# Two queue steps a job in the first output pair, later turns, and a last residual by ScalarE and an accumulating transfer

## The chip, the cores and the metric

The kernel runs on one core of a Trainium2 chip. The metric is the device time of one launch in microseconds. A few terms: TensorE (PE in the profile) multiplies matrices, VectorE (DVE) and ScalarE (ACT) work on elements, GpSimd (POOL) does some small arithmetic and issues DMAs, and SyncE (SP) issues the other DMAs. Each engine works through its own queue of instructions in order. An instruction waits for what it needs, and everything queued behind it on that engine waits too.

## The reference

Two layers, batch 1, 512 tokens (S), 2048 features (D), all in float32:

```python
def hybrid_layer(x, w_in, w_out, g_pre, g_post, ...):
    h = rmsnorm(x, g_pre)
    z = h @ w_in                            # 2048 x 7184
    gq, gk, gv, gg, ga, aq, ak, av, ag = split_columns(z)
    ...
    o_gla = gla_chunk_causal(...)           # 4 heads, gated linear attention
    o_gla = rmsnorm(o_gla, g_gla) * silu(gg)
    o_att = chunk_band_attention(...)       # 8 heads, band of 9 chunks of 64
    o_att = rmsnorm(o_att, g_att) * silu(ag)
    y = concatenate([o_gla, o_att]) @ w_out # 2048 x 2048
    return x + rmsnorm(y, g_post)           # the residual of this case
```

The two large projections, `w_in` and `w_out`, are most of the work.

## The kernel before

**Jobs.** All weights pass through one stream of jobs. A job is one piece of a weight block: 256 input rows by 512 columns, kept as a 128x1024 tile. For each job SyncE loads the piece (512 KB) into `raw` or `H`; where a sum or difference of two pieces is wanted, VectorE forms it (`H` at L185, `raw` at L187); ScalarE makes a rounded high part `wh` (L191); VectorE makes the rest, `wl` (L199). TensorE then multiplies high by high, high by low and low by high: 12 matmuls of 128x512 a job (L381). There are three `wl` tiles and four of each of the other kinds. `ahead` prepares loads, high parts and low parts for the next few jobs after each job's matmuls.

**Pairs.** `fast_gemm` multiplies a pair of weight blocks in seven products of four jobs each instead of eight (P1, P5, P6, P3, P7, P2, P4 in the order of the input pairs; the output pairs have their own order), in the manner of Winograd's form of Strassen's method. It works on sums of the operands (tiles `sa`, loaded from DRAM) as well as on the operands themselves (`a` or `g`). When a product is complete, `finished` calls the pair's consumer once per half of columns and pair of token tiles. The consumer gets a sum, formed by VectorE at L338 from TensorE's accumulator and a kept copy `ev` (L333).

**Side work.** What isn't a job stands in two lists: `tasks`, generators that do one step at a time, and `delayed`, entries with a counter of steps. `pump(n)` advances both by n steps. A `Pace` object calls it after every job with a given rate, so rate 1 is one step a job and rate 3 three. `until` and `drain` pump out of turn.

**The gate pair and the first output pair.** The last pair of input blocks (`PAIRS[5]`) gives the GLA gate. `gg_consume` applies SiLU on ScalarE, multiplies the normalised head outputs on VectorE (L1249; tiles `bias` and `sg`), and puts one `turn_gla` per head and half in `delayed`. A turn transposes the head's output on TensorE (L1164), and splits it into high and low parts on ScalarE and VectorE (L105, L106). The turned parts are operands of the output projection; the task `output_sums` forms their sums and stores them to DRAM. The pair W01 (columns 0 to 1023 of `w_out`) follows in both layers, at rate 1, with consumer `out_consume(0)`. In layer 0 the pair W23 then goes through `std_gemm`, in layer 1 (the last) through `fast_gemm` at rate 3, with `lag=3`.

**Residual.** `project` squares and sums the projected row on ScalarE (L1280) and multiplies it by the gain on VectorE (L1281). When all 2048 columns of a token tile t (128 tokens) are there, `finish_token` reduces the sums on VectorE (L1294), takes them to the power -1/2 on GpSimd (`rsqrt`, L421), and forms x + r*y on VectorE in one step a half (L1306), in place over the loaded residual. It then stores the row (L1308). In the last layer, tokens 0 and 1 are finished by the task `finish(0, ...)` while the last product still runs, and 2 and 3 behind it; token 3 goes in four parts of 512 columns, the fourth by ScalarE and GpSimd. `load_tokens` loads the residual from `x_mid`, a DRAM buffer, with GpSimd's queue (L456), after W01: 1024 columns a tile for tokens 0 to 2, and 512 for token 3 (tiles `bias` and `sg`).

**What sets the order.** The program is written without fixed instruction orders: a scheduler that plans by estimated durations sets each engine's queue order within the data dependences and the reuse of tiles.

Of the kernel before, what the change touches and what calls it, by code (L numbers as in the profile page):

```python
# [11 lines left out]
ALU = mybir.AluOpType  # L12
# [3 lines left out]
P = 128  # L16
# [4 lines left out]
NT = S // P  # L21
# [12 lines left out]
def hybrid_trunk(  # L34
# [653 lines left out]
    def layer(l):  # L688
# [471 lines left out]
        def turn_gla(h, p):  # L1160
            ps = aux()
            for f in range(2):
                for tt in range(2):
                    nc.tensor.transpose(  # L1164
                        ps[:, f * 256 + tt * P : f * 256 + (tt + 1) * P],
                        normed[h, p][:, tt, f * P : (f + 1) * P], ident,
                    )
# [72 lines left out]
        def gg_consume(j, h, t, src, comb):  # L1240
            if t == 0:
                until(lambda: len(gla_done) == 4 and (j or {(1, 2), (1, 3)} <= set(og)))
                for i in range(2):
                    out_parts(2 * j + i)
            sg = t2()
            nc.scalar.activation(sg, settled(src, comb), AF.Silu)
            for i in range(2):
                dst = normed[2 * j + i, h][:, t, :]
                nc.vector.tensor_tensor(out=dst, in0=dst, in1=sg[:, i * 256 : (i + 1) * 256], op=ALU.mult)  # L1249
                if t:  # L1250
                    delayed.append([(8 + 3 * i if j else 6 + i if h == 0 else 3 + i), lambda hd=2 * j + i: turn_gla(hd, h)])

        tasks.append(output_sums())
        fast_gemm(l, PAIRS[5], gg_consume, rate=3, after=fetch_operands)
# [30 lines left out]
        def out_evac(n):  # L1285
# [3 lines left out]
                project(o, n, ps, gp)  # L1289
            return f  # L1290

        def finish_token(t, xs):
            s1, r = sm(1), sm(1)
            nc.vector.tensor_reduce(out=s1, in_=ssy[t], axis=mybir.AxisListType.X, op=ALU.add)  # L1294
            rsqrt(r, s1)
            yield
            end = last and t == NT - 1
            step = 512 if end else xs[0].shape[-1]
            for i in range(D // step):
                h, o = i * step // 1024, i * step % 1024  # L1300
                xt, yt = piece(xs, i * step, step), ys[t, h][:, o : o + step]
                if end and i == 3:
                    nc.scalar.activation(yt, yt, AF.Copy, scale=r)
                    nc.gpsimd.tensor_tensor(out=xt, in0=yt, in1=xt, op=ALU.add)
                else:
                    nc.vector.scalar_tensor_tensor(out=xt, in0=yt, scalar=r, in1=xt, op0=ALU.mult, op1=ALU.add)  # L1306
                q = (nc.sync, nc.scalar)[i % 2] if last and t > 1 else nc.gpsimd
                q.dma_start((out if last else x_mid)[t * P : (t + 1) * P, i * step : (i + 1) * step], xt)  # L1308
                yield

        def finish(pair, xs):
            for j in range(2):
                yield from finish_token(2 * pair + j, xs[j])
# [8 lines left out]
        def out_consume(n):  # L1322
            if n:
                gains[:] = [load_gain(n + j, t2()) for j in range(2)]

            def f(j, h, t, src, comb):
# [11 lines left out]
        fast_gemm(l, W01, out_consume(0), rate=1, after=lambda k, c: used.add((k, c)), end=True, ops=O)  # L1338
# [72 lines left out]
```

## Time and profile before

| | |
|---|---|
| median of 3 runs | 1658.23 us (1656.5 to 1661.95) |
| profiled execution | 1657.88 us, span of the trace 1656.1 us |
| mean granted TensorE clock | 0.994 |
| DMA over the span | 256 GB/s, read 371.32 MB, written 53.23 MB |

A row of a timeline has start and duration in us, engine, source line, operation, tiles (out<-in) and sizes, the number of instructions, and in brackets the idle time before them with the tile or transfer that ended it. A row of waits has the waiting instruction, what it waited for, the sum in us, the count and the longest. A row of windows gives a stretch (from:to), its length, and each engine's busy time with its number of instructions, then the granted clock of TensorE, the busy share of the 16 DMA engines and GB/s. Times in brackets of a timeline row are idle time of that engine and not necessarily lost time of the kernel. Issue instructions of DMAs are listed but not counted as busy.

### The profile page before, as it was taken

Reading aid. Unit: us, or ns where it says so; the run is one execution under the profiler, and the core shown is the slowest. Engines: PE = TensorE matmul, PEld = TensorE weight load, DVE = VectorE, ACT = ScalarE, POOL = GpSimd, SP = SyncE. Lnnn points to the kernel's source line nnn. Section 1 sums busy time; section 2 is a strip of 40 time slices with the busy share of each in tenths; the row PEclk is TensorE's granted clock in tenths of the full one; section 3 lists DMA queues with packets and bytes.
Section 4 is the critical chain, followed back from the end, with each engine's and each line's share of the span. In section 5 each row is a group of like instructions: output and inputs, shape, how many; then the busy total and the mean of one; then the engine's idle time right before and its main releaser. Section 6 shows DMA issues by size and latency. Waiting matters only on the chain.

```text
span 1656.1 us, 24554 instructions
## 1 busy us (share of the span) xinstructions
PE 1623.9 (98%) x8986; PEld 1386.1 (84%) x8986; DVE 1260.1 (76%) x1639; ACT 905.3 (55%) x1494; POOL 131.7 (8%) x200
## 2 busy tenths in 40 slices
PE   9999999999999999999999999999999999998996
PEld 7888999998887777788888889999988877776785
DVE  5977677687688769986785676787766878788778
ACT  7554445566554546555773444465665545565442
POOL 0110000000100110001022000000100000012002
PEclk9999999999999999999999999999999999999998
DMA  8898685885859677386689496858768586876975
GB/s 343 272 349 305 220 302 184 295 286 177 302 186 345 214 253 259 104 309 226 219 310 399 141 330 205 299 174 295 243 206 281 201 317 212 288 252 209 350 230 202
DMA packets 130616, 426.17 MB, mean 257 GB/s; under 512 B 14068, under 2 KB 26740, under 8 KB 130496
## 3 DMA queue, kind: packets, MB, share of 16 engines
q1 hardware_dynamic: 113184, 363.99, 63.5%
q0 software_dynamic: 16736, 59.53, 9.7%
q8 instruction: 71, 1.16, 0.3%
q10 hardware_dynamic: 576, 1.08, 0.2%
q14 instruction: 49, 0.40, 0.1%
HBM read 371.32 MB, written 53.23 MB: 256 GB/s over the span
## 4 chain that ended last, share of the span: by engine, by line
PE 88%; DVE 5%; DMA 3%; issue 2%; ACT 0%; POOL 0%; DVEq 0%; ACTq 0%; POOLq 0%
PE mm L381 42%; PE mm L371 18%; PE mm L302 16%; DMA raw<-in_w_dram 3%; PE ax L891 2%; DVE wl L199 2%; PE ax L381 1%; PE ax L1072 1%; PE ax L874 1%; PE ax L711 1%; PE ax L1044 1%; DVE H L185 1%; PE ax L855 1%; PE ax L854 1%; PE ax L853 1%
## 5 line engine op out<-in xcount | busy, mean ns | idle before, releaser
L381 PE MATMUL mm<-wh,sa 128*128 128x512 f32 x1472 | 479.5, 396 | 4.0 <-ACT wh L191 4.0
L191 ACT CAST wh<-raw 128x1024 fp32r<-128x1024 f32 (+1 forms) x253 | 265.0, 1052 | 245.5 <-PE mm L381 63.1
L199 DVE TENSOR_TENSOR wl<-raw,wh 128x1024 fp32r<-128x1024 f32 (+1 forms) x253 | 306.6, 1215 | 97.5 <-PE mm L381 40.8
L191 ACT CAST wh<-H 128x1024 fp32r<-128x1024 f32 x240 | 251.6, 1051 | 235.3 <-PE mm L381 94.7
L199 DVE TENSOR_TENSOR wl<-H,wh 128x1024 fp32r<-128x1024 f32 x240 | 292.3, 1220 | 95.7 <-PE mm L381 30.0
L381 PEld LDWEIGHTS mm<-wh,sa 128*128 128x128 f32 x1472 | 277.1, 189 | 72.5 <-issue 8.3
L381 PE MATMUL mm<-wl,sa 128*128 128x512 f32 x736 | 290.1, 394 | 5.6 <-DVE wl L199 5.5
L371 PE MATMUL mm<-sa,wh 128*128 128x256 f32 x1280 | 236.8, 285 | 0.5 <-DMA sa<-S 0.5
L381 PE MATMUL mm<-wh,a 128*128 128x512 f32 x608 | 201.3, 396 | 0.0
L371 PEld LDWEIGHTS mm<-sa,wh 128*128 128x128 f32 x1280 | 199.6, 191 | 0.7 <-ACT wh L191 0.6
L371 PE MATMUL mm<-sa,wl 128*128 128x256 f32 x640 | 181.4, 283 | 0.5 <-DVE wl L199 0.5
L381 PEld LDWEIGHTS mm<-wl,sa 128*128 128x128 f32 x736 | 139.1, 189 | 35.5 <-DVE wl L199 8.5
L185 DVE TENSOR_TENSOR H<-H,raw 128x1024 f32<-128x1024 f32 x132 | 160.1, 1217 | 8.5 <-DMA raw<-in_w_dram 7.4
L381 PEld LDWEIGHTS mm<-wh,a 128*128 128x128 f32 x608 | 113.8, 189 | 23.5
L381 PE MATMUL mm<-wl,a 128*128 128x512 f32 x304 | 120.4, 396 | 3.9 <-DVE wl L199 3.9
L187 DVE TENSOR_TENSOR raw<-H,raw 128x1024 f32<-128x1024 f32 x60 | 73.4, 1224 | 65.7 <-DMA raw<-in_w_dram 65.6
L371 PEld LDWEIGHTS mm<-sa,wl 128*128 128x128 f32 x640 | 122.5, 191 | 1.0 <-DVE wl L199 0.7
L421 POOL TENSOR_TENSOR sm<-sm,mhalf 128x2 f32<-128x2 f32 (+2 forms) x42 | 52.7, 1255 | 793.8 <-DVE sm L901 452.8
L371 PE MATMUL mm<-a,wh 128*128 128x256 f32 x512 | 95.2, 285 | 0.0
L381 PE MATMUL mm<-wh,g 128*128 128x512 f32 x288 | 92.2, 395 | 0.0
L302 PE MATMUL mm<-wh,a 128*128 128x512 f32 x288 | 91.7, 390 | 0.0
L333 ACT COPY ev<-mm 128x512 f32<-128x512 f32 x96 | 55.7, 583 | 50.7 <-PE mm L381 33.9
(236 smaller groups left out, 2435.0 us busy)
## 6 DMA issues: line engine op xcount, KB each, us to landing
raw<-in_w_dram SPq DMA_DIRECT2D x323, 512.0 KB, 4.8
sa<-S SPq DMA_DIRECT2D x184, 512.0 KB, 4.3
H<-in_w_dram SPq DMA_DIRECT2D x60, 512.0 KB, 4.7
sa<-A SPq DMA_DIRECT2D x48, 512.0 KB, 6.0
S<-g POOLq DMA_DIRECT2D x32, 512.0 KB, 9.3
sa<-oS SPq DMA_DIRECT2D x16, 512.0 KB, 5.2
oa<-g POOLq DMA_DIRECT2D x12, 512.0 KB, 6.3
bias<-in_rel_dram SPq DMA_DIRECT2D x16, 256.0 KB, 3.2
```

Of the source, the lines that this page charges most:

```text
L185: nc.vector.tensor_tensor(out=h, in0=h, in1=r, op=ALU.add)
L187: nc.vector.tensor_tensor(out=r, in0=h, in1=r, op=ALU.subtract)
L191: last_cast[0] = nc.scalar.copy(self.wh[:, z, :], src[:, z, :]).ins
L199: nc.vector.tensor_tensor(out=self.wl[:, z, :], in0=self.src[:, z, :], in1=self.wh[:, z, :].bitcast(F32), op=ALU.subtract)
L302: nc.tensor.matmul(pss[o], a(part, kk, o) if callable(a) else a[:, part, t], rhs[:, kk, :], start=(i == 0 and kk == 0 and m == 0), stop=(i ...
L333: nc.scalar.copy(e, src[t])
L371: nc.tensor.matmul(dst, lhs[:, kk, f], a[:, part, tok], start=(fresh and kk == 0 and m == 0 and ft % 2 == 0), stop=(c == 3 and kk == 1 and ...
L381: nc.tensor.matmul(out_ps[t], a[:, part, tok], rhs[:, kk, :], start=(fresh and kk == 0 and m == 0), stop=(c == 3 and kk == 1 and m == 2), ...
L421: nc.gpsimd.tensor_tensor(out=out_r, in0=v, in1=mhalf[:, : v.shape[-1]], op=ALU.pow)
L711: nc.tensor.matmul(ps[0:96, half * 256 : (half + 1) * 256], wga[kt // 10][:, kt % 10, :], op[:, i, (kt % 2) * 256 : (kt % 2 + 1) * 256], s ...
L853: nc.tensor.matmul(ps[:, :n], self.qh[:, t], self.kh[:, :n], start=True, stop=False)
L891: nc.tensor.matmul(o, self.pt[i][:, j * P : (j + 1) * P], av[hd // 4, j // 2][:, j % 2, (hd % 4) * P : (hd % 4 + 1) * P], start=(j == 0), ...
```

## The change

Three things change.

1. The turns of the gate pair: their step counts become 8 for the first head of a pair and 11 for the second, in every half; before these were 8 and 11 only for heads 2 and 3, and 6 and 7, or 3 and 4, for heads 0 and 1.
2. The pair W01 advances the side work by two steps a job instead of one, in both layers.
3. In the last layer, tokens 0 and 1 (both halves) and the first half of token 2 are scaled by r in place by ScalarE (L1305 of the changed kernel). A DMA from GpSimd's queue adds the row of `x_mid` to it (L1306), and SyncE stores it (L1307). The loads of x_mid of tokens 0 and 1, four of 512 KB, are dropped; those of tokens 2 and 3 stay. Both tokens 2 and 3 are reduced first (L1296). Then VectorE does the second half of token 2, held behind the reduction of token 3 by `issue_after`, and all four parts of token 3 (L1311).

```diff
-                    delayed.append([(8 + 3 * i if j else 6 + i if h == 0 else 3 + i), lambda hd=2 * j + i: turn_gla(hd, h)])
+                    delayed.append([8 + 3 * i, lambda hd=2 * j + i: turn_gla(hd, h)])
...
-            nc.vector.tensor_reduce(out=s1, in_=ssy[t], axis=mybir.AxisListType.X, op=ALU.add)
+            reduced[t] = nc.vector.tensor_reduce(out=s1, in_=ssy[t], axis=mybir.AxisListType.X, op=ALU.add).ins
             rsqrt(r, s1)
             yield
-            end = last and t == NT - 1
-            step = 512 if end else xs[0].shape[-1]
+            step = 512 if t == NT - 1 else 1024
             for i in range(D // step):
                 h, o = i * step // 1024, i * step % 1024
-                xt, yt = piece(xs, i * step, step), ys[t, h][:, o : o + step]
-                if end and i == 3:
+                yt = ys[t, h][:, o : o + step]
+                rows = slice(t * P, (t + 1) * P), slice(i * step, (i + 1) * step)
+                if last and (t < 2 or (t == 2 and i == 0)):
                     nc.scalar.activation(yt, yt, AF.Copy, scale=r)
-                    nc.gpsimd.tensor_tensor(out=xt, in0=yt, in1=xt, op=ALU.add)
+                    nc.gpsimd.dma_start(yt, x_mid[rows], accum_op=ALU.add)
+                    nc.sync.dma_start(out[rows], yt)
                 else:
-                    nc.vector.scalar_tensor_tensor(out=xt, in0=yt, scalar=r, in1=xt, op0=ALU.mult, op1=ALU.add)
-                q = (nc.sync, nc.scalar)[i % 2] if last and t > 1 else nc.gpsimd
-                q.dma_start((out if last else x_mid)[t * P : (t + 1) * P, i * step : (i + 1) * step], xt)
+                    xt = piece(xs, i * step, step)
+                    with tc.issue_after(reduced[3]) if last and t == 2 else nullcontext():
+                        nc.vector.scalar_tensor_tensor(out=xt, in0=yt, scalar=r, in1=xt, op0=ALU.mult, op1=ALU.add)
+                    q = (nc.sync, nc.scalar)[i % 2] if last else nc.gpsimd
+                    q.dma_start((out if last else x_mid)[rows], xt)
                 yield
...
                     if (j, h) == (0, 1):
-                        for _ in finish_token(o, xs[1][t]):
-                            pass
+                        ends.append(finish_token(o, xs[1][t]))
+                        next(ends[-1])
+                        if t:
+                            for end in ends:
+                                for _ in end:
+                                    pass
...
-        fast_gemm(l, W01, out_consume(0), rate=1, ...)
+        fast_gemm(l, W01, out_consume(0), rate=2, ...)
         drain()
-        xs.extend(load_tokens(half, x_src, nc.gpsimd) for half in range(2))
+        xs.extend(None if last and half == 0 else load_tokens(half, x_src, nc.gpsimd) for half in range(2))
```

The order of instructions moves in three places. The first is TensorE's queue in layer 0 at the end of the gate pair. Its last jobs write `mm_...`; jobs that write `ax_...` with operand `g_...` belong to W01; rows from `cst` are a turn's transposes. Before:

```order
L381 MATMUL mm_6653<-wh_6589,a_1119_5935 128x512
L381 MATMUL mm_6654<-wh_6589,a_1119_5935 128x512
L1164 MATMUL ax_6593<-cst,bias_6053 128x128
L1164 MATMUL ax_6629<-cst,sg_6227 128x128
L1164 MATMUL ax_6593<-cst,bias_6053 128x128 x3
L1164 MATMUL ax_6629<-cst,sg_6227 128x128 x3
L381 MATMUL mm_6653<-wl_6615,a_1119_5935 128x512
```

And now:

```order
L381 MATMUL mm_6629<-wh_6589,a_1119_5935 128x512
L381 MATMUL mm_6630<-wh_6589,a_1119_5935 128x512
L1164 MATMUL ax_6619<-cst,bias_6053 128x128
L1164 MATMUL ax_6651<-cst,sg_6227 128x128
L381 MATMUL ax_6661<-wh_6551,g_1221_6394 128x512
L381 MATMUL ax_6662<-wh_6551,g_1221_6394 128x512
L381 MATMUL ax_6661<-wl_6587,g_1221_6394 128x512
...
L381 MATMUL ax_6662<-wh_6607,g_1226_6423 128x512
L1164 MATMUL ax_6619<-cst,bias_6053 128x128 x3
L1164 MATMUL ax_6651<-cst,sg_6227 128x128 x3
L381 MATMUL mm_6629<-wl_6605,a_1119_5935 128x512
```

A whole job of W01 (12 matmuls with `wh_6551` and `wl_6587`) and the first two matmuls of its next job now stand between the first two transposes and the other six. The matmul with `wl_6605`, which was `wl_6615`, comes after them. Layer 1 has the same move at the same place.

The second is VectorE's queue in layer 1, at the end of the gate pair and the start of W01. L338 forms a sum out of an accumulator, L1281 is the gain, L106 is part of a turn or of `output_sums`. Before:

```order
L185 TENSOR_TENSOR H_14427<-H_14427,raw_14652 128x1024
L338 TENSOR_TENSOR t_2866_14743<-ax_14503,ev_14609 128x512
L1281 TENSOR_TENSOR a_2868_14747<-t_2866_14743,bias_14494 128x512
L338 TENSOR_TENSOR t_2870_14751<-ax_14504,ev_14611 128x512
L199 TENSOR_TENSOR wl_14695<-H_14427,wh_14674 128x1024
L106 TENSOR_TENSOR g_2856_14679<-g_2789_14363,g_2856_14679 128x512
L1281 TENSOR_TENSOR a_2872_14755<-t_2870_14751,bias_14494 128x512
L185 TENSOR_TENSOR H_14482<-H_14482,raw_14676 128x1024
L199 TENSOR_TENSOR wl_14719<-H_14482,wh_14698 128x1024
```

And now:

```order
L185 TENSOR_TENSOR H_14417<-H_14417,raw_14652 128x1024
L338 TENSOR_TENSOR t_2866_14743<-ax_14469,ev_14609 128x512
L185 TENSOR_TENSOR H_14457<-H_14457,raw_14676 128x1024
L1281 TENSOR_TENSOR a_2868_14747<-t_2866_14743,bias_14552 128x512
L338 TENSOR_TENSOR t_2870_14751<-ax_14470,ev_14611 128x512
L199 TENSOR_TENSOR wl_14695<-H_14417,wh_14674 128x1024
L106 TENSOR_TENSOR g_2856_14679<-g_2789_14363,g_2856_14679 128x512
L1281 TENSOR_TENSOR a_2872_14755<-t_2870_14751,bias_14552 128x512
L199 TENSOR_TENSOR wl_14719<-H_14457,wh_14698 128x1024
```

The sum that needs the load `raw_14676` stood behind `wl_14695` and both gains; it now stands ahead of them.

The third is ScalarE's queue in the last product of the last layer. `wh` rows are casts for the last four jobs, L1280 is the square of a projected row. Before:

```order
L1280 ACTIVATE t_3048_15569,ssy_14745<-t_3047_15567 128x512
L191 COPY wh_15600<-H_15013 128x1024
L1280 ACTIVATE t_3050_15574,ssy_14753<-t_3049_15572 128x512
L191 COPY wh_15627<-H_15069 128x1024
L191 COPY wh_15646<-H_15105 128x1024
L191 COPY wh_15665<-H_15181 128x1024
```

And now, with `sm_15570` and `sm_15599` the powers of tokens 0 and 1 from GpSimd:

```order
L191 COPY wh_15594<-H_15013 128x1024
L1280 ACTIVATE t_3046_15566,ssy_14753<-t_3045_15564 128x512
L1305 ACTIVATE a_2868_14747<-a_2868_14747,sm_15570 128x1024
L1305 ACTIVATE g_2991_15303<-g_2991_15303,sm_15570 128x1024
L191 COPY wh_15623<-H_15069 128x1024
L1305 ACTIVATE a_2872_14755<-a_2872_14755,sm_15599 128x1024
L1305 ACTIVATE g_2994_15309<-g_2994_15309,sm_15599 128x1024
L191 COPY wh_15642<-H_15105 128x1024
L191 COPY wh_15661<-H_15173 128x1024
```

Four scalings stand between the casts, two ahead of `wh_15623` and two ahead of `wh_15642`. On VectorE the four residual steps that stood between the last `wl` rows are gone. On GpSimd each power is now followed by its accumulating transfers; the one for token 2 comes after both last powers.

More of the change, by code (lines that the diff above doesn't have):

```diff
@@ L1290, in out_evac @@
             return f
+        reduced = {}
         def finish_token(t, xs):
             s1, r = sm(1), sm(1)
[L1294 removed]
+            reduced[t] = nc.vector.tensor_reduce(out=s1, in_=ssy[t], axis=mybir.AxisListType.X, op=ALU.add).ins
             rsqrt(r, s1)
             yield
[L1297 to L1298 removed]
+            step = 512 if t == NT - 1 else 1024
             for i in range(D // step):
                 h, o = i * step // 1024, i * step % 1024
[L1301 to L1302 removed]
+                yt = ys[t, h][:, o : o + step]
+                rows = slice(t * P, (t + 1) * P), slice(i * step, (i + 1) * step)
+                if last and (t < 2 or (t == 2 and i == 0)):
                     nc.scalar.activation(yt, yt, AF.Copy, scale=r)
[L1304 to L1308 removed]
+                    nc.gpsimd.dma_start(yt, x_mid[rows], accum_op=ALU.add)
+                    nc.sync.dma_start(out[rows], yt)
+                else:
+                    xt = piece(xs, i * step, step)
[3 more added lines that the diff above has]
+                    q.dma_start((out if last else x_mid)[rows], xt)
                 yield
@@ L1312, in finish @@
             for j in range(2):
-                yield from finish_token(2 * pair + j, xs[j])
+                yield from finish_token(2 * pair + j, xs and xs[j])
             if not last:
@@ L1324, in out_consume @@
                 gains[:] = [load_gain(n + j, t2()) for j in range(2)]
+            ends = []
             def f(j, h, t, src, comb):
@@ L1333, in f @@
                     if (j, h) == (0, 1):
-                        for _ in finish_token(o, xs[1][t]):
-                            pass
+                        ends.append(finish_token(o, xs[1][t]))
[4 more added lines that the diff above has]
+                                    pass
             return f
-        fast_gemm(l, W01, out_consume(0), rate=1, after=lambda k, c: used.add((k, c)), end=True, ops=O)
+        fast_gemm(l, W01, out_consume(0), rate=2, after=lambda k, c: used.add((k, c)), end=True, ops=O)
         drain()
-        xs.extend(load_tokens(half, x_src, nc.gpsimd) for half in range(2))
+        xs.extend(None if last and half == 0 else load_tokens(half, x_src, nc.gpsimd) for half in range(2))
         if last:
```

## The prediction

> **What bounds the kernel now.** The page comes first: busy time by engine, the kinds of instruction that feed TensorE, and then the list of what TensorE waits for.
>
> ```profile
> PE 1623.9 (98%) x8986; PEld 1386.1 (84%) x8986; DVE 1260.1 (76%) x1639; ACT 905.3 (55%) x1494; POOL 131.7 (8%) x200
> L191 ACT CAST wh<-raw 128x1024 fp32r<-128x1024 f32 (+1 forms) x253 | 265.0, 1052 | 245.5 <-PE mm L381 63.1
> L199 DVE TENSOR_TENSOR wl<-H,wh 128x1024 fp32r<-128x1024 f32 x240 | 292.3, 1220 | 95.7 <-PE mm L381 30.0
> PE mm L381 <- DVE wl L199: 13.3, 12, 2.1
> PE mm L381 <- ACT wh L191: 4.0, 3, 2.1
> ```
>
> TensorE is busy for 1623.9 of 1656.1 us. The change takes no matmul away, so it can only win in the 32 us in which TensorE stands still, or where it runs at half pace. Of these, 17.3 us are waits for the two halves of a weight block, and the last 12 lie behind the last matmul. So the question is which of those waits fall in the first output pair and in the tail. The timeline of TensorE from the last jobs of the gate pair to the middle of the first output pair shows them, layer 0 first, then layer 1:
>
> ```profile
> 647.38 0.39 PE L381 MATMUL mm<-wh,a 128*128 128x512 f32 x1
> ...
> 651.16 0.55 PE L1164 MATMUL ax<-cst,bias 128*128 128x128 f32 x3 [0.22 <-DVE bias L1249]
> 653.84 0.50 PE L381 MATMUL mm<-wl,a 128*128 128x512 f32 x1 [1.79 <-DVE wl L199]
> 687.09 0.50 PE L381 MATMUL mm<-wl,sa 128*128 128x512 f32 x1 [2.10 <-DVE wl L199]
> 691.72 0.74 PE L381 MATMUL mm<-wh,sa 128*128 128x512 f32 x2 [1.56 <-ACT wh L191]
> 700.22 0.39 PE L381 MATMUL mm<-wl,g 128*128 128x512 f32 x1
> 1473.54 0.50 PE L381 MATMUL mm<-wl,a 128*128 128x512 f32 x1 [1.79 <-DVE wl L199]
> 1508.44 0.50 PE L381 MATMUL mm<-wl,sa 128*128 128x512 f32 x1 [2.01 <-DVE wl L199]
> 1514.69 0.74 PE L381 MATMUL mm<-wh,sa 128*128 128x512 f32 x2 [2.11 <-ACT wh L191]
> 1515.95 0.80 PE L381 MATMUL mm<-wl,sa 128*128 128x512 f32 x1 [0.52 <-DVE wl L199]
> 1525.77 0.39 PE L381 MATMUL mm<-wl,g 128*128 128x512 f32 x1
> ```
>
> Both layers have the same three stalls: 1.79 us between the gate pair's last jobs, 2.0 to 2.1 us at the first wl of the third product, and 1.6 to 2.1 us at the wh after that. VectorE's own windows over these stretches, and what VectorE waits for in them, say how much could be had:
>
> ```profile
> 652.57:687.09 34.52, 32.02 (x43) 1.00 0.47 153
> 686.95:700.22 13.27, 11.41 (x13) 1.00 0.16 47
> 1472.29:1508.44 36.15, 32.19 (x43) 0.95 0.63 212
> 1508.44:1525.77 17.33, 11.72 (x13) 0.80 0.56 209
> DVE wl L199 <- ACT g L105: 1.6, 1, 1.6
> DVE H L185 <- DMA raw<-in_w_dram: 2.7, 1, 2.7
> ```
>
> The columns are length, VectorE's busy time and instructions, granted clock, share of DMA and GB/s. VectorE, not TensorE, is nearly full here: its idle time is 34.52 - 32.02 = 2.50 and 1.86 us in layer 0 (4.36 in all), and 3.96 and 5.61 us in layer 1 (9.57). No reordering gains more than that here while VectorE's work stays what it is.
>
> **Part 1: the first output pair at two steps a job, turns later.** Neither edit adds or drops an engine's work; they reorder. TensorE now runs a whole job of the output pair, 12 matmuls, before the six remaining transposes and the wl that it waited 1.79 us for. The cover costs nothing: its weight block is one that both kernels need.
>
> Layer 0. The early stall of 0.22 + 1.79 us is filled by that job. What decides after it is VectorE's queue up to the wl at 687.09. Of the 2.50 us of idle time there, 1.61 were a wait for ScalarE's copy of a turn (L105); the turns now come later, behind weight blocks that stand ready, so I let this go and keep the rest, a wait for a sum in TensorE. That is 1.6 us. Of the following 1.86 us, a wait for wh, I take a quarter, 0.4. Sum: **2.0 us** (ends 1.0, part of the first alone, and 4.4, all idle time).
>
> Layer 1. The first stretch is built alike: **2.0 us**. The second takes 1525.77 - 1508.44 = 17.33 us where layer 0's (687.09 to 700.22) takes 13.13 for the same jobs. The excess of 4.2 us has three sources in the rows: a DMA wait of 2.67 us on VectorE, wh late by 0.55 us more than in layer 0 (2.11 against 1.56) with 0.52 us of wl behind it, and a granted clock of 0.80. If the weight blocks run ahead, layer 0 shows what the stretch costs, so I take the **4.2 us**. It is the softest term (0 to 4.2): in the changed order the sum H that waited for that DMA stands ahead of another wl on VectorE, so that the same late load would now hold more.
>
> The dropped loads of x_mid belong here. Two of the six rows of such loads, their landing times, and the stretch they fall in:
>
> ```profile
> 1525.53 0.53 POOL L456 DMA_DIRECT2D g<-x_mid  x1
> 1527.51 0.53 POOL L456 DMA_DIRECT2D g<-x_mid  x1 [0.24 <-issue]
> g<-x_mid POOLq DMA_DIRECT2D x6, 512.0 KB, 9.4
> 1526.00:1563.00 37.00, 34.19 (x146) 26.52 (x144) 28.53 (x31) 17.07 (x26) 3.26 (x7) 1.00 0.99 375
> ```
>
> From 1526 to 1563 the DMA engines are full (0.99, 375 GB/s) and TensorE is idle for 37.00 - 34.19 = 2.8 us. Four loads of 512 KB go in all, two of them here: 1.05 MB at 375 GB/s is 2.8 us less to move. The weight loads share the path only in part and the stretch ends full anyway; I take **0.8** of the 2.8 us. Layer 1 in all: 2.0 + 4.2 + 0.8 = **7.0 us** (ends 2.0 and 9.6 + 2.8 = 12.4).
>
> **Part 2: the last layer's residual.** In the last jobs TensorE, VectorE and GpSimd look like this:
>
> ```profile
> 1631.09 0.50 PE L381 MATMUL mm<-wl,g 128*128 128x512 f32 x1 [2.11 <-DVE wl L199]
> 1635.53 0.40 PE L381 MATMUL mm<-wl,g 128*128 128x512 f32 x1
> 1638.62 0.50 PE L381 MATMUL mm<-wl,g 128*128 128x512 f32 x1 [0.17 <-DVE wl L199]
> 1643.52 0.39 PE L381 MATMUL mm<-wh,g 128*128 128x512 f32 x1
> 1627.36 1.28 DVE L1306 SCALAR_TENSOR_TENSOR g<-a,sm,g 128x1024 f32<-128x1024 f32 x1 [0.47 <-POOL sm L421]
> 1629.82 1.21 DVE L199 TENSOR_TENSOR wl<-H,wh 128x1024 fp32r<-128x1024 f32 x1
> 1624.17 3.15 POOL L421 TENSOR_TENSOR sm<-sm,mhalf 128x1 f32<-128x1 f32 x1 [55.62 <-DVE sm L1294]
> 1648.78 0.54 POOL L421 TENSOR_TENSOR sm<-sm,mhalf 128x1 f32<-128x1 f32 x1 [2.73 <-DVE sm L1294]
> ```
>
> VectorE stops 0.47 us for GpSimd's power, does two residual steps (2 x 1.28), and only then the wl that TensorE waits 2.11 us for. Four such steps leave VectorE before the last matmul, about 5 us. TensorE can win 2.11 + 0.17 us; and the 12 matmuls after the first stall take 1635.53 - 1631.09 = 4.44 us, where the 22 from 1638.62 to 1643.52 start 0.23 us apart, which makes 2.8 for 12: 1.6 us lost. Together 3.9. But ScalarE's scalings (its price by the nearest row, a cast of the same size, is 1.05 us) now stand in ScalarE's queue ahead of three wh casts, and wait for the power. VectorE no longer stops for that power: it took 3.15 us under back-to-back VectorE steps against 0.54 alone. I take half, **2.0 us** (ends -0.9 and 3.9).
>
> The Trainium skill, "SBUF — State Buffer", section Who interferes with whom, says that a VectorE instruction with two SBUF inputs contends with a GpSimd instruction that reads SBUF, and that the second fully blocks. By that rule the power waits for one VectorE step at most, 1.22 us, and with its own 0.54 would be there 1.4 us sooner than in 3.15: the sum below would be 1646.3. The 3.15 us are more than two such steps, so the measured wait is the longer one.
>
> Behind the last matmul. Before: from 1643.91 to the end at 1656.1, 12.2 us. After, the branch of token 2's first half is: sums and the power, about 2.1 us (1645.12 + 0.93 in the rows below), scaling 1.05, the accumulating transfer issued behind the last power, so about 3.9 us after the last matmul, its landing, then and the store from SyncE.
>
> ```profile
> 1645.12 0.93 POOL L421 TENSOR_TENSOR sm<-sm,mhalf 128x1 f32<-128x1 f32 x1 [6.85 <-DVE sm L1294]
> 1649.35 1.42 DVE L1306 SCALAR_TENSOR_TENSOR bias<-g,sm,bias 128x512 f32<-128x512 f32 x2 [0.72 <-POOL sm L421]
> 1652.46 0.33 SPq L1308 DMA_DIRECT2D out_dram<-sg  x1
> out_dram<-g POOLq DMA_DIRECT2D x4, 512.0 KB, 3.0
> out_dram<-sg SPq DMA_DIRECT2D x1, 256.0 KB, 2.6
> ```
>
> No row has an accumulating transfer. Its bounds are the nearest rows: 3.0 us for a plain 512 KB from GpSimd's queue in this tail, 9.4 for the load of x_mid under full DMA. I take 5, nearer the first, because the tail's DMA engines are mostly free. From the last landing before, 1652.46 + 2.6, it is 1.04 us to the end. Then 3.9 + 5 + 3.0 + 1.04 = 12.94, against 12.19: **-0.8 us** (ends +1.2, with a landing of 3.0, and -5.1, with 9.4). The other branch, token 3 in four steps of VectorE, ends sooner: power at about 3, four steps of 0.7 (half of 1.42), issue 0.3, landing 2.6, end 1.0, in all 10 us.
>
> The Trainium skill, "DMA: Bandwidth & Descriptors", says that an accumulating transfer reads its destination and writes it later, which speaks for more than a plain transfer's time; no run here shows one.
>
> Sum: 2.0 + 7.0 + 2.0 - 0.8 = 10.2 us from the profiled 1657.88 us: **1647.7 us**. The median of the three runs, 1658.23, lies 0.35 above the profiled execution. 0.3% is 5.0 us, about what a measurement of this kernel can tell from no change: faster means under 1652.9, slower over 1662.9.
>
> **The rivals.** *The pair stays full.* Part 1 gains only 1.0 in layer 0 and 2.0 in layer 1, because VectorE has no less work and the late load now stands ahead of a wl: 3.0 + 2.0 - 0.8 = 4.2, **1653.7 us**. For it: VectorE's 32 busy of 34.5 us. Against: its idle time has named causes that the new order moves away from.
>
> *GpSimd's power holds ScalarE.* Three wh casts wait behind scalings that wait for a power of 3.15 us or more. The tail then stalls that long instead of 2.11 + 0.17, 0.9 us worse than before, and the 2.0 are lost: 1647.7 + 2.9 = **1650.6 us**. For it: the 3.15 us. Against: two of the other powers took 0.54 and 0.93. This is where the rule on shared SBUF reads, above, would bite.
>
> *The accumulating transfers run one behind another (slower).* There are five on GpSimd's queue. The first can be issued about 15 us ahead of the last matmul (power done at 1627.3, scaling 1.05, matmul at 1643.5); with a us each in series, the last lands 5a - 15 us behind it, and store and end add 4.0. At a = 6.3 the end is 20.5 us behind the last matmul and the 11 us from TensorE's stalls are about spent; over 7.3 it is slower by over 0.3%; at 9.4 the end lies 36 us behind, 36 - 12.2 - 11.0 = 12.8 later, **1671 us**. For it: the 9.4 us of x_mid's loads. Against: these were issued 2 us apart and landed 9.4 us later, so they overlapped.
>
> **How the numbers follow.** The forecast, 1643 to 1652, has 0.56; the power on ScalarE 0.13 (also faster); the full pair 0.16, of which 0.03 just under 1652.9; the serial transfers 0.14; 0.01 for no effect at all. Faster 0.56 + 0.13 + 0.03 = 0.72, slower 0.14, same 0.14. The range goes from 1641 (layer 1 or the tail at its better end) to 1657 (the full pair with a landing of 8 us), leaving the slower case out.
>
> **What would show it.** Right: the 1.79 us stalls ahead of wl gone in both layers, layer 1's stretch from the third product near 13 us, no 2.11 us stall by the last residual steps, and some 13 us from last matmul to end. Wrong: those stalls come back under other names, wh or a raw load; ScalarE idle for GpSimd's sm just ahead of a cast; accumulating transfers that land over 6 us after issue or strictly one after another; or an end over 15 us behind the last matmul.

## The result, and the profile after

The changed kernel takes 1646.1 us (median of 4 runs, 1642.34 to 1647.04), the kernel before 1660.09 us (4 runs). The ratio is 0.9917, with a 95% interval of 0.9901 to 0.9933: 13.8 us less (11.1 to 16.4). Forecast were 1647.7 us and 10.2 us less. The profiled execution of the changed kernel took 1642.34 us, 3.8 us under its own median, so what its trace gains, 15.6 us of span, is some 2 us more than the medians do.

First the page's line of engines and the waits of TensorE in the changed kernel:

```profile
PE 1617.2 (99%) x8986; PEld 1383.7 (84%) x8986; DVE 1253.5 (76%) x1635; ACT 909.7 (55%) x1498; POOL 134.2 (8%) x196
PE mm L381 <- DVE wl L199: 5.0, 3, 2.3
PE mm L381 <- ACT wh L191: 1.0, 2, 0.5
```

The waits for a weight part fall from 17.3 to 6.0 us. TensorE's timeline at the places shown of before, both layers:

```profile
655.15 0.48 PE L381 MATMUL mm<-wl,a 128*128 128x512 f32 x1
683.11 0.73 PE L381 MATMUL mm<-wh,sa 128*128 128x512 f32 x2 [0.51 <-ACT wh L191]
686.17 0.50 PE L381 MATMUL mm<-wl,sa 128*128 128x512 f32 x1 [2.33 <-DVE wl L199]
1471.89 0.48 PE L381 MATMUL mm<-wl,a 128*128 128x512 f32 x1
1499.85 0.73 PE L381 MATMUL mm<-wh,sa 128*128 128x512 f32 x2 [0.51 <-ACT wh L191]
1502.90 0.50 PE L381 MATMUL mm<-wl,sa 128*128 128x512 f32 x1 [2.33 <-DVE wl L199]
1538.12 0.50 PE L381 MATMUL mm<-wl,g 128*128 128x512 f32 x1 [0.31 <-DVE wl L199]
```

The first row of each layer is the wl that took 1.79 us to wait for: it now has no bracket. The stall at the first wl of the third product is still there, 2.33 us in both layers. The kernel before has six short waits between 1536 and 1565, 3.1 us in all:

```profile
1537.20 0.50 PE L381 MATMUL mm<-wl,sa 128*128 128x512 f32 x1 [0.39 <-DVE wl L199]
1545.57 0.50 PE L381 MATMUL mm<-wh,sa 128*128 128x512 f32 x1 [0.34 <-ACT wh L191]
1546.83 0.50 PE L381 MATMUL mm<-wl,sa 128*128 128x512 f32 x1 [0.53 <-DVE wl L199]
1550.83 0.50 PE L381 MATMUL mm<-wl,g 128*128 128x512 f32 x1 [0.95 <-DVE wl L199]
1557.17 0.50 PE L381 MATMUL mm<-wl,g 128*128 128x512 f32 x1 [0.60 <-DVE wl L199]
1563.69 0.50 PE L381 MATMUL mm<-wl,a 128*128 128x512 f32 x1 [0.33 <-DVE wl L199]
```

What is left of them is 0.31 us. VectorE's window over layer 0's stretch says why the third product's stall stays:

```profile
639.80:690.20 50.40, 50.34 (x69) 0.98 0.48 157
```

VectorE is busy for 50.34 of 50.40 us. Its idle time is gone, as hoped, and it is now the bound without a gap.

Shorter waits are only part of the gain. TensorE's idle time over the span falls from 32.2 us (1656.1 - 1623.9) to 23.3 (1640.5 - 1617.2), which is 8.9 of the 15.6 us; the other 6.7 are the same 8986 matmuls in less busy time. The stretch from the first wl of layer 1's third product on shows both. These are windows of TensorE over the same matmuls, but for a missing record, of before, of the changed kernel and of turns_only (an experiment below: the later turns alone):

```profile
1508.44:1525.77 17.33, 14.70 (x48) 0.80 0.56 209
1502.90:1515.53 12.63, 12.62 (x49) 0.86 0.56 204
1498.93:1510.76 11.83, 11.31 (x49) 1.00 0.68 252
```

Busy time and granted clock go together: 14.70 us at 0.80, 12.62 at 0.86, 11.31 at 1.00. Slow matmuls follow some stalls and not others. Twelve matmuls at full pace take 2.8 us; behind the stall of 2.01 us at 1508.44 of before they take 4.9, behind the two of 2.33 us 4.0 and 4.4 in the changed kernel, and 4.2 and 2.9 in pair_only. So a stall can cost twice its length, and single traces differ by that. What decides it, these runs don't show.

Where the time went can be read from the traces by comparing the same matmul. The table below gives, for each stage, how much longer (+) or shorter (-) it takes than in the trace of before. Matmuls are counted back from the last one; a few records are missing, so a number may be off by 0.5 us. The stages of before: A to 369.05, B from there to the end of layer 0's first output pair (732.96), C to 1190.79, D to the 320th matmul from the end (1566.32), E to the last matmul's end (1643.91), F to the end of the span (1656.1). A and C hold nothing that the change touches.

| kernel | A | B | C | D | E | F | span |
|---|---|---|---|---|---|---|---|
| changed | +0.6 | -1.8 | -1.6 | -11.2 | -4.9 | +3.3 | -15.6 |
| pair_only | +0.4 | -2.5 | -1.7 | -5.4 | -0.1 | +0.1 | -9.4 |
| rate_only | +0.5 | +2.2 | +0.1 | -1.8 | -1.7 | 0.0 | -0.6 |
| turns_only | +0.8 | -4.0 | +0.1 | -12.5 | -0.4 | 0.0 | -16.0 |
| turns_h1 | +0.3 | -4.1 | -2.0 | -10.5 | -0.4 | 0.0 | -16.6 |
| turns_h0 | +2.1 | +3.6 | -1.3 | -2.1 | +0.6 | 0.0 | +2.8 |
| tail_only | +1.3 | +2.3 | -0.9 | -5.7 | -2.9 | +4.0 | -1.9 |
| loads_kept | +0.7 | -2.3 | -0.3 | -9.4 | -2.2 | +3.9 | -9.7 |
| plain_load | +0.6 | -2.5 | +2.1 | -11.1 | -4.4 | +1.8 | -13.6 |
| turns_tail | +0.5 | -3.7 | -1.1 | -12.2 | -1.8 | +3.3 | -15.0 |
| t2_vector | +1.7 | -1.3 | -1.3 | -10.6 | -4.7 | -0.3 | -16.5 |
| turns_tail_t2v | +0.5 | -4.0 | -1.6 | -12.8 | -3.1 | +1.2 | -19.9 |
| turns_12 | +1.8 | -0.7 | -0.9 | -8.4 | -4.2 | -0.3 | -12.7 |

A and C differ from trace to trace by -2.0 to +2.1 us with the same code, so a single stage of a single trace says nothing under 2 us; groups of rows do.

### The profile page after: what moved, and what is told of

The parts are those of the page before. It is cut to its first block, busy times and chain, and to the rows that moved or that the text cites. A ratio compares the mean times of both kernels' runs of the same rounds, so it can differ in the third digit from the quotient of the medians.

```text
span 1640.5 us, 24563 instructions
## 1 busy us (share of the span) xinstructions
PE 1617.2 (99%) x8986; PEld 1383.7 (84%) x8986; DVE 1253.5 (76%) x1635; ACT 909.7 (55%) x1498; POOL 134.2 (8%) x196
## 4 chain that ended last, share of the span: by engine, by line
PE 94%; DMA 2%; DVE 2%; issue 1%; ACT 0%; SPq 0%; DVEq 0%; POOL 0%; ACTq 0%
PE mm L381 47%; PE mm L371 19%; PE mm L302 16%; PE ax L891 2%; PE ax L381 2%; DMA raw<-in_w_dram 1%; PE ax L1072 1%; PE ax L874 1%; PE ax L711 1%; PE ax L1044 1%; DVE wl L199 1%; PE ax L855 1%; PE ax L854 1%; PE ax L853 1%; PE ax L1164 0%
## 5 line engine op out<-in xcount | busy, mean ns | idle before, releaser
L381 PEld LDWEIGHTS mm<-wh,a 128*128 128x128 f32 x608 | 113.2, 188 | 23.3
L421 POOL TENSOR_TENSOR sm<-sm,mhalf 128x2 f32<-128x2 f32 (+2 forms) x42 | 57.1, 1360 | 791.8 <-DVE sm L901 453.3
```

What stands on the lines that cost most here:

```text
L381: nc.tensor.matmul(out_ps[t], a[:, part, tok], rhs[:, kk, :], start=(fresh and kk == 0 and m == 0), stop=(c == 3 and kk == 1 and m == 2), ...
L421: nc.gpsimd.tensor_tensor(out=out_r, in0=v, in1=mhalf[:, : v.shape[-1]], op=ALU.pow)
```

## The experiments

Each edit is against the kernel named. Times are medians, with the ratio to the kernel before, run beside it on the same chip (medians 1658.32, 1658.27 and 1659.11 us for the three groups of four). The groups ran on different chips, so across groups the ratios are the safer comparison. "Us less" is worked out from the ratio.

**The parts apart: pair_only, tail_only, rate_only, turns_only.**

```diff
 turns_only: before, with
-  delayed.append([(8 + 3 * i if j else 6 + i if h == 0 else 3 + i), ...
+  delayed.append([8 + 3 * i, ...
 rate_only: before, with
-  fast_gemm(l, W01, out_consume(0), rate=1, ...
+  fast_gemm(l, W01, out_consume(0), rate=2, ...
 pair_only: before, with both
 tail_only: the changed kernel, with both undone
```

> Only the output pair's two steps a job and the later turns; the residual as before. Theory A (the gain in the stretch 1526 to 1563 comes from the dropped loads of x_mid): faster than before by 9 to 10 us (1.8 in layer 0, 7.9 in layer 1), and the short stalls between 1526 and 1565, 3.1 us in all, stay. Theory B (these stalls go because the pair's own transfers now run earlier): faster by 13 to 14 us, and those stalls are gone here too. Theory C (the full pair of the prediction): 3 us.

> Only the last residual's change, with the dropped loads; rate 1 and early turns. Theory A: faster than before by 5.4 us (4.0 from the dropped loads, 4.7 from TensorE's last jobs, 3.3 given back behind the last matmul). Theory B: 1 to 2 us (4.7 less 3.3). In both, some 15.5 us from the last matmul to the end where before has 12.2.

> Only two steps a job; turns at their old step counts. Theory A (the later turns fill the early stall, the rate alone only brings turns and sums sooner and so keeps VectorE full): within 2 us of before, the two stalls of 1.79 us stay. Rival (the rate is what empties VectorE's queue ahead of the third product): faster by 6 us or more.

> Only the later turns; one step a job. Theory A: the two early stalls of 2.0 us go, 4 us faster, but the turns now come 8 to 11 jobs later at one step a job, so that their sums may be late for the products that read them: between 6 us faster and 4 slower. Rival (the turns do all of it): faster by 9 us or more, as with the pair's two edits together.

| kernel | median us (runs) | ratio (interval) | us less |
|---|---|---|---|
| pair_only | 1646.6 (5) | 0.9931 (0.9919 to 0.9943) | 11.4 |
| tail_only | 1653.82 (11) | 0.9973 (0.9962 to 0.9984) | 4.5 |
| rate_only | 1658.5 (12) | 1.0004 (0.9993 to 1.0016) | -0.7 |
| turns_only | 1641.45 (4) | 0.9899 (0.9886 to 0.9911) | 16.8 |

The surprise is turns_only: the later turns alone gain more than the whole change. Theory A gave them 6 us at most and fell; the rival, 9 us or more, came in. Two steps a job alone do nothing that shows, as theory A of rate_only said, and beside the later turns they cost 5.3 us; the two intervals (0.9886 to 0.9911 with one step, 0.9919 to 0.9943 with two) don't touch. Rate_only keeps both early stalls:

```profile
654.29 0.50 PE L381 MATMUL mm<-wl,a 128*128 128x512 f32 x1 [1.79 <-DVE wl L199]
1476.35 0.50 PE L381 MATMUL mm<-wl,a 128*128 128x512 f32 x1 [1.79 <-DVE wl L199]
```

The price of the two steps shows at the third product. These are the stalls of turns_only nearest to it, to be held against 0.51 + 2.33 us in each layer of the changed kernel (and of pair_only, where the four rows have the same idle times):

```profile
689.60 0.50 PE L381 MATMUL mm<-wl,sa 128*128 128x512 f32 x1 [0.92 <-DVE wl L199]
1507.87 0.50 PE L381 MATMUL mm<-wl,sa 128*128 128x512 f32 x1 [0.52 <-DVE wl L199]
```

VectorE's queue shows the cause. The row that TensorE waited 2.33 us for is the eleventh wl counted from the one at the early stall. First VectorE's windows from that wl to the start of the eleventh, of the changed kernel; then the eleventh's own row:

```profile
653.14:684.90 31.76, 31.70 (x42) 1.00 0.50 161
684.90 1.22 DVE L199 TENSOR_TENSOR wl<-H,wh 128x1024 fp32r<-128x1024 f32 x1
```

The same two views of turns_only:

```profile
653.31:680.78 27.47, 27.47 (x35) 1.00 0.50 169
680.78 1.22 DVE L199 TENSOR_TENSOR wl<-H,wh 128x1024 fp32r<-128x1024 f32 x1
```

At two steps a job, 42 instructions stand ahead of the eleventh wl, at one step 35, and VectorE has next to no idle time in either. The seven more are side work brought forward: four at L106 (turns and `output_sums`), two sums out of an accumulator (L338) and a gain (L1281). They make the part 4.3 us later.

Of pair_only's theories, A fell: the stalls between 1526 and 1565 are gone, though the four loads are still there. That is what B said, but the 13 to 14 us that it gave with it are not reached in the median. Here the two steps a job help. These are TensorE's windows over that stretch, of before, pair_only and turns_only:

```profile
1525.77:1563.69 37.92, 34.78 (x147) 1.00 0.99 376
1521.65:1554.74 33.09, 33.09 (x148) 1.00 1.00 382
1510.76:1548.27 37.51, 34.87 (x147) 1.00 1.02 396
```

In pair_only TensorE has no idle time with the DMA engines as full as before (1.00); with the later turns at one step a job it still waits 2.6 us. The same matmuls take 33.1 to 35.1 us in the five kernels with both edits (changed, pair_only, loads_kept, plain_load, t2_vector), 36.5 to 38.9 in the four with later turns at one step (turns_only, turns_h1, turns_tail, turns_tail_t2v), and 35.4 to 37.7 in the three with early turns (tail_only, turns_h0, rate_only). So with the later turns the two steps give back some 3.5 us here of what they cost ahead of it, and are a loss only on balance.

Tail_only gains 4.5 us, nearer its theory A (5.4) than B (1 to 2); from the last matmul to the end it takes 16.2 us. On top of the later turns at one step, the same edit gives 0.5 us by the ratios (turns_tail below against turns_only). The table of stages shows where the two overlap: stage D gains 5.7 us in tail_only, but 12.2 in turns_tail against 12.5 in turns_only.

**The tail: turns_tail, t2_vector, turns_tail_t2v, plain_load.**

```diff
 turns_tail: the changed kernel, with
-  fast_gemm(l, W01, out_consume(0), rate=2, ...
+  fast_gemm(l, W01, out_consume(0), rate=1, ...
 t2_vector: the changed kernel, with
-  if last and (t < 2 or (t == 2 and i == 0)):
+  if last and t < 2:
 turns_tail_t2v: the changed kernel, with both of these
 plain_load: the changed kernel, with
-  nc.gpsimd.dma_start(yt, x_mid[rows], accum_op=ALU.add)
+  nc.gpsimd.dma_start(yt, x_mid[rows])
```

> The changed kernel with the output pair at one step a job again. Theory A (two steps a job push sums of the output operands ahead of weight parts in VectorE's full queue): the stalls of 0.51 and 2.33 us at the third product go in both layers, and it takes 1639 to 1641 us, 5 us less than the change. Rival (the two steps are a cost only without the last residual's change): 1646 us, like the change.

> The changed kernel with the first half of token 2 on VectorE again, so that no accumulating transfer starts behind the last matmul; the queue orders are otherwise the same. Theory A (that transfer, 8 us from issue to the store behind it, sets the end): 15.5 us from last matmul to end become 11 to 12, and the time 1642 us. Rival (the stores of tokens 0 and 1 ahead of it on SyncE are as late): 15 us, no change against 1646.

> Both: one step a job, later turns, the residual of tokens 0 and 1 by ScalarE and accumulating transfers, token 2 by VectorE. If both theories hold, 1636 to 1638 us, less than the turns alone (1641.45). If the tail's gain is only chance, 1641.

> The changed kernel with each of the five accumulating transfers made a plain load of the same bytes on the same queue, so the scaled rows of tokens 0, 1 and half of 2 are overwritten by the residual. Theory A (accumulating is what is dear): issue to store falls from 5.6 to 10.2 us to some 3 to 4, and the end comes 3 to 4 us sooner, 1642 us. Rival (the price is that of GpSimd's queue and of the DMA engines at that time): the same 6 to 10 us and 1646.

| kernel | median us (runs) | ratio (interval) | last matmul to end |
|---|---|---|---|
| turns_tail | 1641.23 (5) | 0.9896 (0.9875 to 0.9916) | 15.6 |
| t2_vector | 1644.05 (6) | 0.9915 (0.9894 to 0.9936) | 11.9 |
| turns_tail_t2v | 1638.01 (5) | 0.9879 (0.9858 to 0.9900) | 13.4 |
| plain_load | 1644.15 (6) | 0.9907 (0.9887 to 0.9926) | 13.9 |

What the fifth accumulating transfer does is clear from the rows. In the changed kernel, the last matmul, the issue of that transfer, and the store that waits for it:

```profile
1624.61 0.39 PE L381 MATMUL mm<-wh,g 128*128 128x512 f32 x1
1628.70 0.88 POOL L1306 DMA_DIRECT2D g<-x_mid  x1 [1.04 <-ACT g L1305]
1636.66 0.33 SPq L1307 DMA_DIRECT2D out_dram<-g  x1
```

It is issued 3.7 us after the last matmul's end, and 8.0 us pass from the start of its issue to the store; in tail_only, loads_kept and turns_tail it is 8.0 us too. With plain_load, which leaves out the addition, the same rows are:

```profile
1628.17 0.39 PE L381 MATMUL mm<-wh,g 128*128 128x512 f32 x1
1632.19 0.57 POOL L1306 DMA_DIRECT2D g<-x_mid  x1 [0.96 <-ACT g L1305]
1637.75 0.33 SPq L1307 DMA_DIRECT2D out_dram<-g  x1
```

Here 5.6 us pass, in one trace. So of the 8.0 us, some 2.4 are the price of adding, and 5.6 that of a plain load of 512 KB on this queue while the other stores run: theory A had the sign, the rival most of the size. The 2.4 are rough, since the store ahead of it on SyncE goes out 0.9 us before this transfer in the changed kernel and 5.0 us before it here; for the four transfers of tokens 0 and 1 the difference is 1.3 to 3.0 us. In t2_vector the last matmul starts at 1627.36, and the last stores are issued at 1634.43 (SyncE) and 1635.10 (ScalarE):

```profile
1627.36 0.39 PE L381 MATMUL mm<-wh,g 128*128 128x512 f32 x1
1634.43 0.33 SPq L1313 DMA_DIRECT2D out_dram<-sg  x1
1635.10 0.34 ACTq L1313 DMA_DIRECT2D out_dram<-sg  x1
```

The end is back at 11.9 us, what theory A said. The gain of 3.6 us behind the last matmul is 2.0 in the median, 1644.05 against 1646.1 from another group, and 0.3 by the ratios: the whole time doesn't show it. One step a job in the full change (turns_tail) is 4.9 us less by the medians and 3.5 by the ratios, and its intervals overlap a little too (0.9875 to 0.9916 against 0.9901 to 0.9933); that two steps cost is shown by pair_only against turns_only. In turns_tail the stalls of 0.51 and 2.33 us are gone, as theory A said; 0.92 and 0.50 us are left a little later. Both edits together (turns_tail_t2v) make the fastest kernel of this study, 1638.01 us, at the upper end of the 1636 to 1638 expected and 20.3 us less than before, and its interval ends where that of the changed kernel begins. It has 13.4 us behind the last matmul where t2_vector has 11.9. Its last store is issued as soon, 7.4 us after the last matmul's end in both, and lands later. The last store of tokens 0 and 1 goes out 3.7 us ahead of it, in t2_vector 5.3; that this makes them land later is not shown.

**Loads and turns: loads_kept, turns_h1, turns_h0, turns_12.**

```diff
 loads_kept: the changed kernel, with
-  xs.extend(None if last and half == 0 else load_tokens(half, ...
+  xs.extend(load_tokens(half, ...
 turns_h1: before, with
-  (8 + 3 * i if j else 6 + i if h == 0 else 3 + i)
+  (8 + 3 * i if j or h else 6 + i)
 turns_h0: before, with
-  (8 + 3 * i if j else 6 + i if h == 0 else 3 + i)
+  (8 + 3 * i if j or h == 0 else 3 + i)
 turns_12: turns_tail_t2v, with
-  8 + 3 * i
+  (12 if j == 0 and h else 8) + 3 * i
```

> The changed kernel with the four loads of x_mid for tokens 0 and 1 put back (nothing reads them). Theory A (the dropped loads free the full DMA engines after the third product): 3 to 4 us slower than the change, 1649 to 1650 us, and short waits for wl and wh of 2 us or more in all between the third product and the last pair. Rival (the order on VectorE frees that stretch): 1646 us.

> From the kernel before: only the turns of the second half of heads 0 and 1 are later (8 and 11 for 3 and 4), those of the first half stay at 6 and 7. Theory A (the last turns, which come due at the pair's first jobs, are what stands ahead of weight parts in VectorE's queue): most of the 16.8 us of all later turns, 12 us or more, 1646 us or less. Rival (the first half's): 4 us or less.

> The other part: the first half's turns at 8 and 11 for 6 and 7, the second half's stay at 3 and 4. Theory A: 4 us or less, 1654 us or more, the early stalls of 1.79 us stay. Rival: 12 us or more.

> The fastest version so far (one step a job, later turns, token 2 on VectorE; 1638.0 us) with the second half's turns of heads 0 and 1 later still, at 12 and 15 steps. Theory A (VectorE's queue ahead of the third product is what they must stay out of): the stalls of 0.92 and 0.5 us at the third product go too, 1635 to 1638 us. Rival (the sums that are made of these turns are then late for the later products): a new wait for sa or wl behind the third product, 1640 us or more.

| kernel | median us (runs) | ratio (interval) |
|---|---|---|
| loads_kept | 1647.32 (6) | 0.9932 (0.9911 to 0.9952) |
| turns_h1 | 1643.14 (6) | 0.9913 (0.9894 to 0.9932) |
| turns_h0 | 1656.66 (12) | 0.9987 (0.9973 to 1.0002) |
| turns_12 | 1646.39 (6) | 0.9934 (0.9914 to 0.9954) |

The four entries that moved from 3 and 4 to 8 and 11 steps, two in each layer, gain 14.4 us by themselves. The first half's gain 2.2 us, with an interval from -0.3 to 4.5, and keep the early stalls:

```profile
655.88 0.60 PE L381 MATMUL mm<-wl,a 128*128 128x512 f32 x1 [2.13 <-DVE wl L199]
1479.44 0.80 PE L381 MATMUL mm<-wl,a 128*128 128x512 f32 x1 [2.13 <-DVE wl L199]
```

Later still is too late. With 12 and 15 steps (turns_12), TensorE waits at the third product for the sums made of these turns:

```profile
689.54 0.79 PE L381 MATMUL mm<-wh,sa 128*128 128x512 f32 x1 [2.99 <-ACT sa L105]
1507.76 0.50 PE L381 MATMUL mm<-wh,sa 128*128 128x512 f32 x1 [3.09 <-ACT sa L105]
```

So the rival was right there: 8.4 us slower than turns_tail_t2v by the medians, 9.1 by the ratios, with intervals that don't touch. Of the step counts tried for the second half's turns, 8 and 11 are the best: there the turns are behind the weight parts of the early jobs and still in time for the third product.

Loads_kept is not told apart from the change by time (1.2 us by the medians, 2.5 by the ratios, intervals overlapping). In its trace the loads do not bring back the waits between the third product and the last pair (theory A's place). What comes is a pair of waits 6 us behind the third product's first wl. Just ahead of them VectorE waits for a weight load (first row):

```profile
1508.54 1.23 DVE L185 TENSOR_TENSOR H<-H,raw 128x1024 f32<-128x1024 f32 x1 [1.03 <-DMA raw<-in_w_dram]
1510.97 0.73 PE L381 MATMUL mm<-wh,sa 128*128 128x512 f32 x2 [1.07 <-ACT wh L191]
1512.40 0.50 PE L381 MATMUL mm<-wl,sa 128*128 128x512 f32 x1 [0.69 <-DVE wl L199]
```

That the loads of x_mid made this one late is not shown: tail_only, without these loads, waits 0.91, 0.52 and 1.74 us in the same product.

Stage D tells a little more. With the turns later and two steps a job, it gains 10.6 to 11.2 us without the loads (changed, t2_vector, plain_load) and 5.4 and 9.4 with them (pair_only, loads_kept). But pair_only's 5.4 holds a wait for an `sa` tile that stands far ahead of the loads:

```profile
1343.09 0.47 PE L381 MATMUL mm<-wh,sa 128*128 128x512 f32 x1 [2.92 <-DMA sa<-S]
```

Without it, it would be 8.3. At one step a job the gain is 12.2 and 12.8 without the loads and 10.5 and 12.5 with; with early turns it is 5.7 without (tail_only) and 1.8 and 2.1 with (rate_only, turns_h0). The loads cost some 0 to 4 us there; the runs don't settle it closer.

## Why the prediction was right, and where it wasn't

The range held the result and the likeliest case came in: 1647.7 us forecast and 1646.1 measured, 10.2 us less forecast and 13.8 measured. By its own steps:

- **The early stall** of 0.22 + 1.79 us is gone in both layers, by the job of the output pair that now covers it. Right. It is the turns of the second half that do it (turns_h1), not the two steps.
- **Layer 0, 2.0 us**: the trace has 1.8. The 1.61 us wait for L105 went, with all other idle time of VectorE. But the stall at the third product stayed, and the two steps are why: with the later turns and without the two steps, stage B gains 3.7 to 4.1 us in four traces. TensorE's idle time in stage B falls by 2.9 us; slower matmuls behind the 2.33 us stall (granted clock 0.86, before 1.00) take 1.1 of it back.
- **Layer 1, 7.0 us**: 11.2 in the trace, inside the ends of 2.0 and 12.4. The first stretch gave 2.7 (2.0 forecast). The second, from the third product, took 12.6 us where 13 were forecast, 4.7 less (4.2 forecast). The step that failed is the 0.8 us for the stretch from 1526 to 1563, taken as DMA-bound: it gave 3.9. Its six short waits go with the two steps and the later turns together, loads or no loads: pair_only has none of them at a DMA share of 1.00. Of the 11.2, the loads may be 0 to 4.
- **The first output pair as one part.** The prediction credited two steps a job and the later turns together. This is the step that was wrong in kind: the turns gain 16.8 us and the two steps take 5.3 of it back. VectorE's windows, 32.02 us busy of 34.52, were quoted there; what was missed is that more steps a job put more work in front of the weight parts in a queue that has no room.
- **TensorE's last jobs, 2.0 us**: 4.9 in this trace. The seven other traces with the new residual gain 1.8 to 4.7 in stage E, the five with the old one -0.6 to 1.7. The means of the two groups, 3.5 (with this trace) and 0.4, put about 3 us to it. The mechanism of the rival, ScalarE held by the power, came true without harm:

```profile
1607.89 3.15 POOL L421 TENSOR_TENSOR sm<-sm,mhalf 128x1 f32<-128x1 f32 x1 [54.19 <-DVE sm L1296]
1611.08 1.16 ACT L1305 ACTIVATE a<-a,sm 128x1024 f32<-128x1024 f32 x1 [2.64 <-POOL sm L421]
1613.18 1.03 ACT L191 CAST wh<-H 128x1024 fp32r<-128x1024 f32 x1
1614.56 1.22 DVE L199 TENSOR_TENSOR wl<-H,wh 128x1024 fp32r<-128x1024 f32 x1
```

ScalarE stood idle for 2.64 us ahead of the scaling, with the cast behind it. Its wl was still made in time, since TensorE shows no wait for it; in the other traces with the new residual TensorE waits 0 to 1.3 us in its last jobs. The power took 3.15 us again, as in eleven of the fourteen traces; in t2_vector, plain_load and turns_12 it took 1.41. By the rule of the Trainium skill ("SBUF — State Buffer", section Who interferes with whom) that was weighed in the prediction it would have waited for one VectorE step, 1.76 us at most with its own 0.54. The 1.41 us agree with that, the 3.15 do not, and the longer wait was the right one to count on.
- **Behind the last matmul, -0.8 us**: -3.3. The step is the landing of the accumulating transfer, taken as 5 us; from the start of issue to the store behind it, it takes 8.0. The end of 9.4 was the nearer one: the transfer runs beside the stores of tokens 2 and 3. The Trainium skill's sentence ("DMA: Bandwidth & Descriptors", section Rules for kernel authors) that such a transfer reads its destination and writes it later agrees in sign: 8.0 against 5.6 us for the plain load in plain_load.
- **The rival of transfers one behind another** was half right. The four of tokens 0 and 1 were issued from 1612.54 to 1617.61, and their stores follow at 1618.16, 1620.90, 1624.46 and 1627.82, about 3 us apart:

```profile
1612.54 0.96 POOL L1306 DMA_DIRECT2D a<-x_mid  x1 [1.50 <-ACT a L1305]
1617.61 0.85 POOL L1306 DMA_DIRECT2D g<-x_mid  x1
1618.16 0.34 SPq L1307 DMA_DIRECT2D out_dram<-a  x1
1620.90 0.34 SPq L1307 DMA_DIRECT2D out_dram<-g  x1
1624.46 0.33 SPq L1307 DMA_DIRECT2D out_dram<-a  x1
1627.82 0.33 SPq L1307 DMA_DIRECT2D out_dram<-g  x1
```

They do queue, but at some 3 us each, under the 6.3 from which the prediction let it decide. Adding is not the main reason: behind the plain loads of plain_load the four stores follow 1.8 to 3.9 us apart. The thresholds themselves were worked out wrongly. By the prediction's own terms the 11 us are spent at 6.8 us each, not 6.3 ((11.0 + 12.2 + 15 - 4.0) / 5), and 0.3% is lost from 7.8, not 7.3; at 3 us nothing hangs on it.

The terms that were too small (layer 1, the last jobs) and the one that was too favourable (the end) offset each other, and the sum came out closer than its parts: that it came within 1.6 us is in part luck. Of the signs named ahead, the right ones came for the early stalls, the 2.11 us stall and layer 1's third product. But three signs of being wrong came with them: ScalarE idle for the power ahead of a cast, an accumulating transfer that takes over 6 us, and 15.5 us from the last matmul to the end, over the 15 named.

## What to carry to other kernels

Where one in-order queue feeds the critical engine and is full, the time at which side work enters that queue matters: here the same work, four turns entered 5 to 7 steps later, gained 14.4 us. Side work that is needed later should be put behind the parts that are needed now, but not so late that it is waited for, as at 12 and 15 steps. Cut a change into its edits before believing in it as a whole: here one edit gained 16.8 us, the second took back 5.3, and the third gave 4.5 alone and 0.5 on top of the first. A transfer that starts behind the last matmul lies on the path with its whole time, here 8.0 us; use such a path only for work that ends well ahead.

## What the runs showed of the hardware

An accumulating transfer of 512 KB from GpSimd's queue behind the last matmul took 8.0 us from issue to the dependent store in four traces, where a plain load at the same place took 5.6 in one, and its issue took GpSimd 0.88 us where the plain one took 0.57. The small power on GpSimd took 3.15 us in eleven traces and 1.41 in three while VectorE ran steps back to back, against 0.54 alone. Behind a TensorE stall of 1.8 to 2.3 us, the next 12 matmuls took from 2.9 us, about full pace, to 5.3.
